# Gates of a hybrid encoder layer by Strassen's seven products

## The chip, the cores and the metric

The kernel runs on one core of one Trainium2 chip. The metric is device time in microseconds of one execution: 1601.31 us, the median of 3 runs (1599.61 to 1603.38). The engines are TensorE (PE; its weight loads are listed as PEld), VectorE (DVE), ScalarE (ACT), GpSimd (POOL) and SyncE (SP, which here only issues transfers).

## The reference

One layer over L = 1040 tokens (16 meta tokens and 1024 real ones) of width 1024, float32. What matters here:

```python
a = rms_norm(h, norm_mix[l])
(q_na, k_na, v_na, q_hg, z_f, z_b, i_hg, g_hg, gate_na, gate_hg) = split_cols(a @ w_in[l])
y_na = neighbourhood_attention(hd(q_na), hd(k_na), hd(v_na), na_rpb[l]).reshape(B, L, NA_WIDTH) @ w_na_out[l]
y_hg = hgrn2_branch(q_hg, z_f, z_b, i_hg, g_hg, lb_all[:, l], hg_norm[l]) @ w_hg_out[l]
mix = jax.nn.sigmoid(gate_na) * y_na + jax.nn.sigmoid(gate_hg) * y_hg
h = h + mix @ w_o[l]
m = rms_norm(h, norm_mlp[l])
h = h + jnp.square(jax.nn.relu(m @ w_up[l])) @ w_down[l]
```

The two gates are 2048 of the 6144 columns of `a @ w_in`. The meta tokens' own outputs are dropped at the end, so the kernel computes the gates for the 1024 real tokens only.

## The kernel before, in words

Everything is float32 in and out. Each large product is made of three matmuls on the float32r type: an operand is split into a rounded high part and the remainder (`split`, L93: a cast on ACT, a subtraction on DVE), and high x high, high x low and low x high are summed in PSUM (`mm3`, L132). A matmul has a 128x128 stationary block and 512 moving columns.

The order of the work is: the norm of x and its transposition into `aT` (two halves of 512 tokens, each a high and a low tile of 8 blocks of 128 input rows, in the pool `up`); four heads of the HGRN2 recurrence (`hgrn`, L265); four pairs of attention heads (L501); gates and branch outputs (L626 to L674); the product with W_o (L693 to L777); the MLP's up projection, already by seven products in Winograd's form (L892 to L937); the MLP's down projection and the final norm.

In the heads, projections of a 128-column block of w_in (`proj_steps`: 2 x 24 matmuls and 2 evacuations) are put between the levels of the recurrence's tree, in which DVE and POOL make the next level's operands (L360 to L364). POOL also adds `kd` (L338) and takes the root before the head's normalisation (L90, L91). Head outputs are kept in `oT` (L454), attention outputs in `OT` (L613), 16 KB per partition each, until the branch outputs split them into `sh` and `sl` (L651).

Gates (`gate_proj`, L632) are 16 column blocks of 2 x 24 matmuls, each half evacuated by a sigmoid on ACT (L636) into one of four tiles `sg`. They run two to four blocks ahead of the branch outputs, which use them: for each of 8 output blocks and 2 halves, 12 matmuls and then a multiplication by the gate (L670; L672 and L673 for the second branch).

Outside the down projection (which is written with a manual order) the framework orders each engine's instructions by readiness and by place in the program, and a tile that takes another's space waits for it. Raw weights, high and low parts of blocks live in the pool `wp` with two slots each. The high and low tiles of W_o (`wrp`) take space at the right end once `oT`, `OT`, `sh` and `sl` are given back, and `mT`, the split of `mix`, lies in the space of `aT`. PSUM has 8 banks: two `mm` banks throughout and six that `psum_pools` deals out again at each stage. All loads and nearly all stores are issued by SP in one queue.

Of the kernel before, what the change touches and what calls it, by code (L numbers as in the profile page):

```python
# [18 lines left out]
P = 128  # L19
# [27 lines left out]
def layer(ctx: ExitStack, tc: tile.TileContext, x, meta, w_in, w_na, w_hg, w_o, w_up, w_dn,  # L47
# [129 lines left out]
    def proj(*args, **kw):  # L177
        for _ in proj_steps(*args, **kw):
            pass
# [85 lines left out]
    def hgrn(hd, hp, lmask_get, gates, more):  # L265
# [3 lines left out]
        def tmp(name):  # L269
            return hp.tile([P, TH], F32, tag="tmp", name=name, bufs=4)  # L270

# [158 lines left out]
        for hf in (1, 0):  # L430
            po = pos[hf] = bank("b", "po")
            for c in range(3, -1, -1):
# [3 lines left out]
                if g < 7:  # L436
                    pe.matmul(po[:, c], QQ[:, 0, g * P:(g + 1) * P], SB[:, g], start=False, stop=True)
        list(more)
        yield
        for hf in (1, 0):  # L440
            po = pos[hf]
            sq = tmp("sq").rearrange("p (c v) -> p c v", v=P)
            act.activation(sq, po, AF.Square)
            ss = hp.tile([P, 4], F32, tag="ss", name="ss", bufs=2)
            dve.tensor_reduce(ss, sq, axis=AX.X, op=ALU.add)
# [12 lines left out]
    with tc.tile_pool(name="hp", bufs=1, reuse_waits="tile") as hp:  # L458
# [20 lines left out]

    OTp = oTs.enter_context(tc.tile_pool(name="OTp", bufs=1, side="right", reuse_waits="tile"))  # L480
    psum_pools(mx=1, s=2, t=2, b=1)
    OT = OTp.tile([P, NPAIR, T], F32, name="OT")
    with tc.tile_pool(name="np", bufs=1, reuse_waits="tile") as npl:
# [17 lines left out]
        for p in range(NPAIR):  # L501
# [51 lines left out]

            po = {}

            def scores(s, i):
# [19 lines left out]
            def values(s, i, js, pr):  # L576
# [34 lines left out]
                dve.tensor_copy(low, ov[64:])  # L611
                dst = OT[64 * i:64 * i + 64, p].rearrange("p (r s c) -> p s r c", s=8, c=8)
                dve.tensor_tensor(dst[:, s - 3:s + 1], ov[:64].rearrange("p s (r c) -> p s r c", c=8),  # L613
# [8 lines left out]
            for st in pend:  # L622
                values(*st)


    psum_pools(mx=3, a=3)  # L626
# [5 lines left out]
    def gate_proj(col):  # L632
        sg = sgp.tile([P, T], F32, tag="sg", name="sg")

        def ev(ps, t0, n):
            act.activation(sg[:, t0:t0 + n], ps, AF.Sigmoid)  # L636
        proj(col, ev)
        return sg

    gates = []  # L640

    def gates_to(n):
        for m in range(len(gates), min(n, 2 * KC)):
            gates.append(gate_proj((C_GH if m < KC else C_GN) + (m % KC) * P))

    for br, (wsrc, src) in enumerate(((w_hg, oT), (w_na, OT))):
        with tc.tile_pool(name="op", bufs=1, reuse_waits="tile") as op_:
            sh = op_.tile([P, 4, T], F32R, name="sh")
            sl = op_.tile([P, 4, T], F32R, name="sl")
            gates_to(8 * br + 2)  # L650
            for k in range(4):  # L651
                split(sh[:, k], sl[:, k], src[:, k])
            for jj in range(0, KC, 2):
                gates_to(8 * br + jj + 4)
                raw = wp.tile([P, KC, P], F32, tag="raw", name="raw").rearrange("p a b -> p (a b)")
                hi = wp.tile([P, KC, P], F32R, tag="hi", name="hi").rearrange("p a b -> p (a b)")
                lo = wp.tile([P, KC, P], F32R, tag="lo", name="lo").rearrange("p a b -> p (a b)")
                sp.dma_start(raw.rearrange("p (k c) -> p k c", k=4),
                             wsrc[:, jj * P:(jj + 2) * P].rearrange("(k p) c -> p k c", p=P))
                split(hi, lo, raw)  # L660
                for j in (jj, jj + 1):
                    sg = gates[8 * br + j]
                    for h in range(2):
                        pm = mm_tile()
                        t = slice(h * TH, (h + 1) * TH)
                        for k in range(4):
                            c = slice(k * 2 * P + (j - jj) * P, k * 2 * P + (j - jj + 1) * P)
                            mm3(pm, hi[:, c], lo[:, c], sh[:, k, t], sl[:, k, t], k == 0, k == 3)
                        if br == 0:
                            dve.tensor_tensor(mix[:, j, t], pm, sg[:, t], op=ALU.mult)  # L670
                        else:
                            dve.tensor_tensor(sg[:, t], pm, sg[:, t], op=ALU.mult)  # L672
                            dve.tensor_tensor(mix[:, j, t], mix[:, j, t], sg[:, t], op=ALU.add)  # L673
    oTs.close()  # L674

# [42 lines left out]
    for i in range(8):  # L718
# [4 lines left out]

    NP = DFF // (2 * P)
    dramp = ctx.enter_context(tc.tile_pool(name="dramp", bufs=1, space=bass.MemoryType.DRAM))
# [5 lines left out]
    def winograd(eng, a11, a12, a21, a22, s1, s2, s3, s4):  # L735
        eng.tensor_tensor(s1, a21, a22, op=ALU.add)
        eng.tensor_tensor(s2, s1, a11, op=ALU.subtract)
        eng.tensor_tensor(s3, a11, a21, op=ALU.subtract)
        eng.tensor_tensor(s4, a12, s2, op=ALU.subtract)

# [54 lines left out]

    def chain(ps, lhs, rhs, first):

        for k in range(4):
            c = slice(k * P, (k + 1) * P)
            pe.matmul(ps, lhs[0][:, c], rhs[0][:, k], start=first and k == 0, stop=False, skip_group_check=True)  # L800
            pe.matmul(ps, lhs[0][:, c], rhs[1][:, k], start=False, stop=False, skip_group_check=True)  # L801
            pe.matmul(ps, lhs[1][:, c], rhs[0][:, k], start=False, stop=k == 3, skip_group_check=True)  # L802


    w_pools = [upa]

    def weights(src):
# [5 lines left out]
        return hi, lo  # L813

    def up_bank(t):
        return bank(t, t).rearrange("p a b -> p (a b)")

# [388 lines left out]
```

## Time and profile before

| | |
|---|---|
| median of 3 runs | 1601.31 us (1599.61 to 1603.38) |
| profiled execution | 1602.57 us, of which the span (first to last instruction) is 1600.4 us |
| mean granted TensorE clock | 0.997 |
| PE / DVE / ACT / POOL busy | 1555.2 / 964.2 / 607.6 / 333.9 us |
| heads | about 40 to 390 us |
| attention | about 390 to 616 us |
| gates and branch outputs | about 616 to 862 us |
| W_o | about 864 to 957 us |
| up projection | about 960 to 1288 us |

Times in the profile are from the span's start. In a group's row stand line, engine, operation, output<-inputs and count, then busy time and the mean of one in ns, then the idle time before it and what ended it. In a row of the timeline stand start, duration and, in brackets, the idle time before it and what ended that. Matmuls overlap, so their pace is read from the distance of their starts.

### The profile page before, as it was taken

Reading aid. Unit: us, or ns where it says so; the run is one execution under the profiler, and the core shown is the slowest. Engines: PE = TensorE matmul, PEld = TensorE weight load, DVE = VectorE, ACT = ScalarE, POOL = GpSimd, SP = SyncE. Lnnn points to the kernel's source line nnn. Section 1 sums busy time; section 2 is a strip of 40 time slices with the busy share of each in tenths; the row PEclk is TensorE's granted clock in tenths of the full one; section 3 lists DMA queues with packets and bytes.
Section 4 is the critical chain, followed back from the end, with each engine's and each line's share of the span. In section 5 each row is a group of like instructions: output and inputs, shape, how many; then the busy total and the mean of one; then the engine's idle time right before and its main releaser. Section 6 shows DMA issues by size and latency. Waiting matters only on the chain.

```text
span 1600.4 us, 20348 instructions
## 1 busy us (share of the span) xinstructions
PE 1555.2 (97%) x7876; PEld 1309.3 (82%) x7876; DVE 964.2 (60%) x1524; ACT 607.6 (38%) x1082; POOL 333.9 (21%) x299
## 2 busy tenths in 40 slices
PE   6999999999999999999999998999999999999998
PEld 5788889888888888888887876788888878887886
DVE  6666767565767865123226258766666454779666
ACT  6221121112656654112123035555555443434444
POOL 4322121212011000000000012543333300227033
PEclk9999999999999999999999999999999999999999
DMA  5101001002122111111412123544444477563324
GB/s 184 40 27 40 27 28 40 27 28 68 30 74 63 45 41 40 40 53 53 145 53 78 54 105 113 168 156 163 145 152 145 160 261 234 199 224 118 99 86 145
DMA packets 120625, 158.03 MB, mean 99 GB/s; under 512 B 6337, under 2 KB 80065, under 8 KB 120529
## 3 DMA queue, kind: packets, MB, share of 16 engines
q1 hardware_dynamic: 118624, 150.70, 28.7%
q10 hardware_dynamic: 1584, 4.98, 0.8%
q8 instruction: 62, 1.02, 0.3%
q0 software_dynamic: 320, 1.05, 0.2%
q14 instruction: 35, 0.28, 0.1%
HBM read 118.96 MB, written 37.75 MB: 98 GB/s over the span
## 4 chain that ended last, share of the span: by engine, by line
PE 86%; DVE 7%; issue 3%; ACT 2%; POOL 1%; DMA 1%; DVEq 0%; POOLq 0%; SPq 0%; ACTq 0%
PE mm L134 14%; PE mm L133 13%; PE mm L135 13%; PE mm L949 4%; PE pa L949 4%; PE pc L949 4%; PE sc L351 4%; PE pb L949 3%; PE pb L800 3%; PE pb L802 3%; PE pb L801 3%; PE pc L800 2%; PE pc L801 2%; PE pc L802 2%; PE pa L800 2%
## 5 line engine op out<-in xcount | busy, mean ns | idle before, releaser
L133 PE MATMUL mm<-aT,hi 128*128 128x512 f32 (+2 forms) x896 | 328.6, 367 | 1.2 <-DVE QX L507 1.2
L135 PE MATMUL mm<-aT,lo 128*128 128x512 f32 (+2 forms) x896 | 327.5, 366 | 0.1
L134 PE MATMUL mm<-aT,hi 128*128 128x512 f32 (+2 forms) x896 | 326.6, 364 | 0.0
L133 PEld LDWEIGHTS mm<-aT,hi 128*128 128x128 f32 x896 | 169.6, 189 | 23.5 <-issue 1.4
L135 PEld LDWEIGHTS mm<-aT,lo 128*128 128x128 f32 x896 | 169.4, 189 | 23.1 <-POOL lo L124 0.3
L134 PEld LDWEIGHTS mm<-aT,hi 128*128 128x128 f32 x896 | 169.5, 189 | 22.0
L95 DVE TENSOR_TENSOR dl<-ur,dh 128x1024 fp32r<-128x1024 f32 x55 | 76.5, 1392 | 93.7 <-ACT dh L94 91.8
L94 ACT CAST dh<-ur 128x1024 fp32r<-128x1024 f32 x55 | 57.9, 1053 | 162.3 <-issue 78.1
L123 ACT CAST hi<-raw 128x1024 fp32r<-128x1024 f32 x44 | 46.3, 1053 | 189.0 <-PE mm L134 171.2
L124 DVE TENSOR_TENSOR lo<-raw,hi 128x1024 fp32r<-128x1024 f32 x42 | 51.6, 1230 | 85.8 <-ACT hi L123 85.8
L90 POOL TENSOR_SCALAR rtm<-ssq 128x1 f32<-128x1 f32 (+1 forms) x17 | 7.5, 439 | 397.0 <-ACT junk L754 372.1
L812 DVE TENSOR_TENSOR wl<-sx,wh 128x512 fp32r<-128x512 f32 x70 | 50.0, 722 | 30.7 <-ACT wh L811 30.7
L811 ACT CAST wh<-sx 128x512 fp32r<-128x512 f32 x70 | 42.6, 620 | 64.9 <-PE pc L801 27.3
L812 DVE TENSOR_TENSOR wl<-raw,wh 128x512 fp32r<-128x512 f32 x46 | 50.2, 1091 | 23.8 <-ACT wh L811 23.0
L351 PE MATMUL sc<-QQ,X 128*128 128x128 f32 x448 | 61.7, 288 | 1.5 <-DVE QQ L378 1.2
L351 PEld LDWEIGHTS sc<-QQ,X 128*128 128x128 f32 x448 | 58.2, 196 | 4.4 <-issue 2.0
L363 POOL TENSOR_TENSOR Y<-X,TN 128x512 f32<-128x512 f32 x20 | 33.8, 1691 | 110.3 <-DVE X L360 110.3
L819 ACT ACTIVATE uv<-uv 128x512 f32<-128x512 f32 x48 | 30.4, 633 | 66.4 <-DVE uv L927 49.9
L932 POOL TENSOR_TENSOR us<-u,uv 128x512 f32<-128x512 f32 x15 | 24.3, 1619 | 137.5 <-ACT uv L820 137.5
L569 DVE CUSTOM_DVE_ANT_0 pr<-nsc,NB 128x432 f32<-128x432 f32 (+1 forms) x64 | 35.3, 559 | 28.1 <-PE nsc L564 27.9
L800 PE MATMUL pb<-nt,wh 128*128 128x512 f32 x128 | 50.3, 393 | 2.0 <-DVE uv L920 2.0
L551 POOL TENSOR_TENSOR NB<-NB,bs 128x256 f32<-128x256 f32 (+1 forms) x24 | 19.6, 842 | 156.3 <-DMA NB<-in_wmask 94.1
(331 smaller groups left out, 3906.3 us busy)
## 6 DMA issues: line engine op xcount, KB each, us to landing
ur<-usp SPq DMA_DIRECT2D x55, 512.0 KB, 3.3
raw<-in_w_in SPq DMA_DIRECT2D x48, 512.0 KB, 3.7
raw<-in_w_up SPq DMA_DIRECT2D x16, 1024.0 KB, 6.0
usp<-us SPq DMA_DIRECT2D x60, 256.0 KB, 2.1
w<-in_w_dn SPq DMA_DIRECT2D x16, 512.0 KB, 4.5
usp<-uv SPq DMA_DIRECT2D x30, 256.0 KB, 2.5
xt<-in_x SPq DMA_DIRECT2D x8, 512.0 KB, 9.3
hres<-in_x SPq DMA_DIRECT2D x8, 512.0 KB, 6.5
```

Source lines behind the costliest of these rows:

```text
L94: act.copy(hi, src)
L95: dve.tensor_tensor(lo, src, hi.bitcast(F32), op=ALU.subtract)
L124: eng.tensor_tensor(lo[:, :kc], raw[:, :kc], hi[:, :kc].bitcast(F32), op=ALU.subtract)
L133: pe.matmul(ps, lh, rh, start=first, stop=False)
L134: pe.matmul(ps, lh, rl, start=False, stop=False)
L135: pe.matmul(ps, ll, rh, start=False, stop=last)
L351: pe.matmul(sc[:, c], X[:, tb + c * P:tb + (c + 1) * P], fap(QQ, tb + c * P, [[2 * h, P // (2 * h)], [T + h, 2], [1, h]]), start=True, sto ...
L800: pe.matmul(ps, lhs[0][:, c], rhs[0][:, k], start=first and k == 0, stop=False, skip_group_check=True)
L801: pe.matmul(ps, lhs[0][:, c], rhs[1][:, k], start=False, stop=False, skip_group_check=True)
L802: pe.matmul(ps, lhs[1][:, c], rhs[0][:, k], start=False, stop=k == 3, skip_group_check=True)
L812: dve.tensor_tensor(v(lo), src, v(hi).bitcast(F32), op=ALU.subtract)
L949: pe.matmul(ps, a[n == 2][:, q, j * P:(j + 1) * P], b[n == 1][:, q], start=first and n == 0, stop=last and n == 2, skip_group_check=True)
```

## The change

**Gates.** The gate matrix (1024 inputs x 2048 outputs) is taken in 8 pairs of 128-column blocks. For a pair, inputs are halved (rows 0 to 511 and 512 to 1023), as are outputs (the pair's two blocks) and tokens (two halves of 512), which makes a 2x2 by 2x2 product of blocks; it is computed with seven block products in Winograd's form, 12 matmuls each, instead of eight. Products 1 and 2 of every pair use plain halves of `a` (`first_gates`); the result of product 1 is kept in `g1`, and the two together are one quarter of the output. The other five (`gate_pair`) use sums of weights, made per pair on DVE (`gate_sums`), and sums of `a`, named t1 to t4. PSUM is dealt as pa, pb and pc, two banks each.

**Sums of `a`.** They are made on POOL, head by head, inside the recurrence (`block_sums`, after the head's last matmuls), from high plus low of the blocks, and stored in DRAM. In the gate stage they are loaded again and split (`second_operand`); t2 takes the place of one quarter of `a`, which is no longer needed.

**Gate results** are no longer kept until used: each quarter is stored in DRAM by a transfer issued on ACT's queue behind the sigmoid (`gate_out`), and loaded by SP in the branch outputs.

**Branch outputs** of the heads and the attention go to DRAM too (the tile `oT` and the large `OT` are gone), and are loaded and split (`branch_operand`) into the space of `a`, after all gates instead of between them. Matmuls, multiplications and weights of the branch outputs stay as they are. `tmp` in the heads has 6 slots instead of 4.

```diff
-    oTs = ExitStack()
-    oTp = oTs.enter_context(tc.tile_pool(name="oTp", bufs=1, side="right"))
-    oT = oTp.tile([P, NHG, T], F32, name="oT")
+    def block_sums(k, pool_):
+        r = {}
+        for v, h, kk in (("t1", 0, k), ("t3", 1, k), ("t2", 1, k + 4), ("t4", 0, k + 4)):
+            r[v] = pool_.tile([P, TH], F32, tag="tmp", name="rt", bufs=6)
+            hi, lo = (t[:, kk, :TH].bitcast(F32) for t in aT[h])
+            pool.tensor_tensor(r[v], hi, lo, op=ALU.add)
+        pool.tensor_tensor(r["t1"], r["t3"], r["t1"], op=ALU.subtract)
+        pool.tensor_tensor(r["t3"], r["t2"], r["t3"], op=ALU.subtract)
+        pool.tensor_tensor(r["t2"], r["t2"], r["t1"], op=ALU.subtract)
+        pool.tensor_tensor(r["t4"], r["t4"], r["t2"], op=ALU.subtract)
+        for v in r:
+            sp.dma_start(tsp[v][k], r[v])
...
         list(more)
+        block_sums(hd, hp)
         yield
...
-            dve.scalar_tensor_tensor(oT[:, hd, hf * TH:(hf + 1) * TH], pt.rearrange("p c t -> p (c t)"),
+            ot = hp.tile([P, TH], F32, tag="ot", name="ot", bufs=2)
+            dve.scalar_tensor_tensor(ot, pt.rearrange("p c t -> p (c t)"),
...
+            sp.dma_start(osp[0][hd][:, hf * TH:(hf + 1) * TH], ot)
...
+            sp.dma_start(osp[1][p], OT)
...
+    def gate_out(c, h, t, src):
+        act.activation(t, src, AF.Sigmoid)
+        act.dma_start(gsp[c][:, h * TH:(h + 1) * TH], t)
+
+    def first_gates(ms):
+        blocks, ps = [], []
+        for m in ms:
+            hi, lo = load_block(w_in[:, gate_col(2 * m):gate_col(2 * m) + P], KC)
+            blocks.append([[flat(t)[:, q * TH:(q + 1) * TH] for t in (hi, lo)] for q in range(2)])
+        for m, b in zip(ms, blocks):
+            ps.append(mm_tile())
+            chain(ps[-1], b[0], aV["b11"], True)
+            act.copy(g1[m], ps[-1])
+        for m, b, p in zip(ms, blocks, ps):
+            chain(p, b[1], aV["b21"], False)
+            gate_out(2 * m, 0, gfp.tile([P, TH], F32, tag="go", name="go", bufs=2), p)
+
+    psum_pools(pa=2, pb=2, pc=2)
+    first_gates((0, 1))
+    first_gates((2, 3))
...
+    def second_operand(v):
+        for k in range(4):
+            t = g_tile("gv", TH, bufs=5)
+            sp.dma_start(t, tsp[v][k])
+            split(aV[v][0][:, k], aV[v][1][:, k], t)
+
+    def gate_weights(src):
+        w_turn[0] ^= 1
+        n = src.shape[1]
+        hi, lo = (wp.tile([P, KC, P], F32R, tag=t, name=t) if w_turn[0] else
+                  gp.tile([P, KC, P], F32R, tag=t, name=t, bufs=2) for t in ("hi", "lo"))
+        hi, lo = flat(hi)[:, :n], flat(lo)[:, :n]
+        split(hi, lo, src)
+        return [[t[:, q:q + TH] for t in (hi, lo)] for q in range(0, n, TH)]
+
+    def gate_sums(m):
+        raw = []
+        for q in range(2):
+            t = (wp.tile([P, KC, P], F32, tag="raw", name="raw") if m % 2 == 0 else
+                 gp.tile([P, KC, P], F32, tag="raw", name="raw", bufs=2))
+            c = gate_col(2 * m + q)
+            sp.dma_start(t, w_in[:, c:c + P].rearrange("(k p) c -> p k c", p=P))
+            raw.append(flat(t))
+        sa, sb = g_tile("sx", D, bufs=2), g_tile("sx", D, bufs=2)
+        winograd(dve, raw[0][:, :TH], raw[0][:, TH:], raw[1][:, :TH], raw[1][:, TH:],
+                 sb[:, :TH], sa[:, TH:], sb[:, TH:], sa[:, :TH])
+        W = {}
+        W["s4"], W["s2"] = gate_weights(sa)
+        W["s1"], W["s3"] = gate_weights(sb)
+        W["a22"], = gate_weights(raw[1][:, TH:])
+        return W
+
+    def gate_pair(m, W, before):
+        pb, pc = up_bank("pb"), up_bank("pc")
+        p3 = g_tile("p3", TH, bufs=2)
+        chain(pc, W["s4"], aV["b22"], True)
+        act.copy(p3, pc)
+        before()
+        chain(pb, W["s2"], aV["t2"], True)
+        u1, u3, u2 = (g_tile("gv", TH, bufs=5) for _ in range(3))
+        dve.tensor_tensor(u1, pb, g1[m], op=ALU.add)
+        chain(pc, W["s1"], aV["t1"], False)
+        dve.tensor_tensor(u1, u1, pc, op=ALU.add)
+        gate_out(2 * m, 1, u1, u1)
+        chain(pb, W["s3"], aV["t3"], False)
+        dve.tensor_tensor(u3, pb, g1[m], op=ALU.add)
+        pool.tensor_tensor(u3, u3, p3, op=ALU.subtract)
+        dve.tensor_tensor(u3, u3, pc, op=ALU.add)
+        gate_out(2 * m + 1, 1, u3, u3)
+
+        def last():
+            chain(pb, W["a22"], aV["t4"], False)
+            dve.tensor_tensor(u2, pb, g1[m], op=ALU.add)
+            gate_out(2 * m + 1, 0, u2, u2)
+        return last
+
+    W = gate_sums(0)
+    first_gates((4, 5))
+    for v in ("t2", "t1"):
+        second_operand(v)
+    first_gates((6, 7))
+    for v in ("t3", "t4"):
+        second_operand(v)
+    last = lambda: None
+    for m in range(NG):
+        last = gate_pair(m, W, last)
+        if m + 1 < NG:
+            W = gate_sums(m + 1)
+    last()
...
+    osrc = [u_tiles(br, "o") for br in range(2)]
+    def branch_operand(br):
+        for k in range(4):
+            raw = wp.tile([P, KC, P], F32, tag="raw", name="raw")
+            sp.dma_start(flat(raw), osp[br][k])
+            split(*(t[:, 2 * k:2 * k + 2, :TH] for t in osrc[br]), raw.rearrange("p (h a) b -> p h (a b)", h=2))
+
+    branch_operand(0)
+    for br, wsrc in enumerate((w_hg, w_na)):
+        for jj in range(0, KC, 2):
...
+            if br == 0 and jj == 2:
+                branch_operand(1)
+            for j in (jj, jj + 1):
+                sg = sgp.tile([P, T], F32, tag="sg", name="sg")
+                sp.dma_start(sg, gsp[8 * br + j])
```

`chain` (12 matmuls: 4 input blocks times three), `winograd` (four sums) and `up_bank` are the functions that the up projection had; they are defined earlier now.

More of the change, by code (lines that the diff above doesn't have):

```diff
@@ L623, in layer, with winograd, chain @@
                 values(*st)
+            sp.dma_start(osp[1][p], OT)
+    def winograd(eng, a11, a12, a21, a22, s1, s2, s3, s4):
+        eng.tensor_tensor(s1, a21, a22, op=ALU.add)
+        eng.tensor_tensor(s2, s1, a11, op=ALU.subtract)
+        eng.tensor_tensor(s3, a11, a21, op=ALU.subtract)
+        eng.tensor_tensor(s4, a12, s2, op=ALU.subtract)
+    def chain(ps, lhs, rhs, first):
+        for k in range(4):
+            c = slice(k * P, (k + 1) * P)
+            pe.matmul(ps, lhs[0][:, c], rhs[0][:, k], start=first and k == 0, stop=False, skip_group_check=True)
+            pe.matmul(ps, lhs[0][:, c], rhs[1][:, k], start=False, stop=False, skip_group_check=True)
+            pe.matmul(ps, lhs[1][:, c], rhs[0][:, k], start=False, stop=k == 3, skip_group_check=True)
@@ L626, in layer @@
+    W = gate_sums(0)
[11 more added lines that the diff above has]
+    last()
+    gps.close()
+    gfs.close()
     psum_pools(mx=3, a=3)
@@ L646, in layer @@
[L646 to L673, printed above, removed]
@@ L794, in a_tile @@
         return pool_.tile([P, n], dt, tag=tag, name=tag, bufs=bufs)
[L796 to L802, printed above, removed]
     w_pools = [upa]
```

67 lines of the change are left out of this document (44 added, 23 removed).

## The prediction

> **What bounds the kernel now.** I read the engine totals of the page and its chain of waits first, then the busy time stage by stage, then the order of instructions inside the stage that the change rewrites.
>
> ```profile
> span 1600.4 us, 20348 instructions
> PE 1555.2 (97%) x7876; PEld 1309.3 (82%) x7876; DVE 964.2 (60%) x1524; ACT 607.6 (38%) x1082; POOL 333.9 (21%) x299
> ...
> PE 86%; DVE 7%; issue 3%; ACT 2%; POOL 1%; DMA 1%; DVEq 0%; POOLq 0%; SPq 0%; ACTq 0%
> ```
>
> TensorE is the chain for 86% of the span. A busy TensorE need not be at its rate, so the stages and the spacing of matmuls come next (columns of the stages: length, PE, PEld, DVE, ACT, POOL with counts, granted clock, DMA share, GB/s).
>
> ```profile
> 640.00:760.00 120.00, 120.00 (x531) 99.41 (x530) 28.73 (x31) 23.10 (x30) 0.00 (x0) 1.00 0.16 49
> 760.00:866.00 106.00, 104.86 (x463) 86.36 (x462) 42.45 (x58) 25.40 (x37) 0.00 (x0) 1.00 0.24 80
> ...
> 1060.00:1120.00 60.00, 60.00 (x266) 49.69 (x266) 37.82 (x49) 31.02 (x54) 24.16 (x17) 1.00 0.46 157
> ...
> 1300.00:1400.00 100.00, 100.00 (x442) 82.61 (x441) 58.12 (x66) 39.90 (x53) 10.66 (x7) 1.00 0.66 231
> ```
>
> ```profile
> 742.64 0.39 PE L133 MATMUL mm<-sh,hi 128*128 128x512 f32 x1
> ...
> 745.36 0.39 PE L133 MATMUL mm<-sh,hi 128*128 128x512 f32 x1
> ```
>
> The two starts are 12 matmuls apart: 2.72 us, so one 128x512 matmul costs 0.2267 us, whatever the 0.39 us in its row. Gates and branch outputs (640 to 866) are that stream without a hole, at granted clock 1.00, with DVE 24 to 40% busy, ACT 19 to 24%, and POOL empty. A matmul taken out there is time taken out, as long as nothing new makes TensorE wait. The stage at 1060 is the up projection, which has the structure that the gates will get (seven products, L892 to L937), with DVE 63% and ACT 52% busy, and it too has no hole.
>
> **The change, part by part.** *Products.*
>
> ```profile
> L636 ACT ACTIVATE sg<-mm x32: 587/598/601, 615.6 to 841.5; 128x512 f32<-128x512 f32 x32
> ```
>
> 32 half-columns of 24 matmuls are 768. After: 8 pairs of 7 products of 12 are 672. 96 x 0.2267 = **-21.8 us**. The 384 matmuls of the branch outputs stay.
>
> The Trainium skill, "TensorE: Matmul & The Clock Gate", section "Back-to-back issue gap", gives about 131 ns for a sustained N=512 matmul; by it the saving would be an estimated 12.6 us. The 227 ns of the trace is used.
>
> *One pair in steady state.* 5 products remain in it (two are done ahead), 13.6 us of TensorE.
>
> ```profile
> L124 DVE TENSOR_TENSOR lo<-raw,hi x42: 1207/1224/1586, 46.2 to 820.3; 128x1024 fp32r<-128x1024 f32 x42
> L736 DVE TENSOR_TENSOR sx<-raw x16: 679/692/1661, 987.0 to 1238.2; 128x512 f32<-128x512 f32 x16
> L94 ACT CAST wh<-raw x8: 1045/1048/1053, 862.5 to 884.4; 128x1024 fp32r<-128x1024 f32 x8
> L94 ACT CAST mT<-mix x16: 610/620/623, 835.8 to 865.5; 128x512 fp32r<-128x512 f32 x16
> L912 ACT COPY p<-pc x16: 568/580/588, 995.3 to 1269.8; 128x512 f32<-128x512 f32 x16
> L753 ACTq DMA_DIRECT2D hsp<-hres x8: 326/326/337, 915.3 to 957.3; - x8
> ```
>
> DVE: 4 weight sums and 5 evacuations at 0.69, splits of 2 x 1.22 and 0.69: 9.4 us, 69%. ACT: casts 2 x 1.05 and 0.62, one copy 0.58, 3 sigmoids at 0.60, 3 store issues at 0.33: 6.1 us, 45%. A store issued on ACT follows the sigmoid that it stores, so it holds the ACT queue for little more than its issue. This is the load that the up projection carries without a hole, with one POOL operation instead of five. Cost 0; if cover fails, each evacuation that is late costs TensorE about the 2 us seen at 1016 below.
>
> *The start of the stage.* While the first products of blocks 2 to 7 run (6 x 5.44 = 32.6 us; blocks 0 and 1 fill the gaps of the attention's end as the first gate did before), DVE has 6 block splits (7.3), 16 operand splits at 0.69 (11.0) and the first sums and their splits (5.9): 24 us. ACT has 6 x (1.05 + 0.58 + 0.60 + 0.33) + 16 x 0.62 + 2.7 = 28 us. It fits, but two things are narrow. A block's second product ends 2.72 us before its slot's next user must be ready, against sigmoid, cast and the low part (0.60 + 1.05 + 1.22 = 2.9 us). And the pool of two split slots is shared: two of the three splits of the first sums take both slots and hold them until products 3, 5 and 7 of pair 0, so blocks 4 to 7 wait, and pair 0 must run before them, on raw weights whose load starts only when two raw slots are free (3.7 us to landing) and then 2.8 us of sums. The nearest row is the start of the up projection:
>
> ```profile
> raw<-in_w_in SPq DMA_DIRECT2D x48, 512.0 KB, 3.7
> ...
> 960.00:1000.00 40.00, 34.40 (x172) 27.77 (x173) 34.50 (x52) 24.08 (x46) 10.81 (x9) 0.96 0.37 113
> ```
>
> ```profile
> 989.65 0.50 PE L800 MATMUL pb<-nT,wh 128*128 128x512 f32 x1 [3.96 <-ACT wh L811]
> 990.69 0.79 PE L800 MATMUL pc<-nT,wh 128*128 128x512 f32 x1 [0.31 <-ACT wh L811]
> 1016.00 0.50 PE L800 MATMUL pb<-nt,wh 128*128 128x512 f32 x1 [1.97 <-DVE uv L920]
> ```
>
> That slice lost 5.6 of its 40 us, at a granted clock of 0.96 behind the long hole, and the wait at 1016 another 2.0: near 8. DVE was 86% busy there, with transposes that the gates don't have. Bounds 0 and 8; I take **+4.5**, half of it at the raw weights.
>
> *Sums of a.* Per head, 8 POOL operations on 128x512 (4 of hi+lo, 4 differences), then 4 stores on SP. The rows are a group, a wait of POOL, the second head's stage and the lengths (min/median/max) of one DVE line.
>
> ```profile
> L363 POOL TENSOR_TENSOR Y<-X,TN 128x512 f32<-128x512 f32 x20 | 33.8, 1691 | 110.3 <-DVE X L360 110.3
> ...
> POOL st L90 <- DVE ss L445: 120.6, 8, 32.0
> ...
> 155.00:240.00 85.00, 84.46 (x527) 75.22 (x526) 57.93 (x105) 16.66 (x32) 18.91 (x20) 1.00 0.11 32
> ...
> L361 DVE TENSOR_TENSOR X<-X,TN x20: 673/685/1526, 63.8 to 347.9; 128x512 f32<-128x512 f32 x20
> ```
>
> 8 x 1.69 = 13.5 us per head, 54 in all. POOL is 18.9 busy in 85 and once per head idle up to 32.0 us (before L90), so the 13.5 fits. Queued behind it on POOL stand the root before the head's normalisation (L90, L91), the kd sum and the level steps (L338, L363), whose results DVE and TensorE wait for; one operation in the wrong place delays these by 1.7 us, and projections fill. L361 shows a DVE operation stretched from 0.69 to 1.53 us; if all of a head's 13.5 us stretched DVE, it would be 71 of 85 and still not the bound. On SP, weight loads stand behind stores that wait for POOL, but a block is loaded one block (48 matmuls, 10.9 us) ahead. In the first head, before TensorE has projections enough, less is covered. Bounds 0 and 54; by the idle row nearly all hides: **+1.5**.
>
> The Trainium skill, "SBUF — State Buffer", section "Who interferes with whom", says that a VectorE instruction with two SBUF inputs and a GpSimd instruction that reads SBUF block each other whole. The 1.53 us in L361 agrees. It speaks against these sums, and is the third rival's reason.
>
> *Outputs through DRAM.* oT and OT become stores (8 of 256 KB, 4 of 512 KB) and 8 loads of 512 KB into freed space of a; their splits are those made before. Gates add 32 stores of 256 KB and 16 loads of 512 KB. In the branch outputs (384 x 0.2267 = 87 us) this is 12.6 MB more, 145 GB/s on top of 49 to 80: about what the stage at 1300 moves (231) with TensorE full. The gate for the first output can be loaded only after the last product has left its space, 3.7 us like the raw weights, against five banks of 2.72 each. Cost 0; uncovered, one load, 3.7.
>
> *The seam to W_o.* Weights of W_o waited for the space of sh and sl, until the last branch matmul:
>
> ```profile
> 862.09 0.39 PE L135 MATMUL mm<-sh,lo 128*128 128x512 f32 x1
> 863.62 1.43 PE L133 MATMUL mm<-wh,mT 128*128 128x512 f32 x5 [1.14 <-ACT wh L94]
> 872.67 0.50 PE L133 MATMUL mm<-wh,mT 128*128 128x512 f32 x1 [0.24 <-ACT wh L94]
> 873.93 0.50 PE L134 MATMUL mm<-wl,mT 128*128 128x512 f32 x1 [0.28 <-DVE wl L95]
> ```
>
> That pool is gone, so they can be split earlier: **-1.7**, the three waits. Bounds 0 and -2.6: the first seam is 1.53 from start to start, 1.3 beyond the spacing, and some 0.3 is lost around each of the others beside its wait. New there: the second half of mT lies where the W_na operand is read to the end, so its 8 splits (8 x 0.69, 5.5 us) start only then; rows 0 to 3 of W_o (4 x 5.44 = 21.8 us) use the first half and cover it.
>
> *Table.* ACT changes from Exp to Sigmoid once, 1.28 us. Gate results no longer wait for attention's space, so a sigmoid may slip between exponentials and cost two more changes. ACT is 61% busy there:
>
> ```profile
> L636 ACT ACT_TABLE_LOAD  x1: 1283/1283/1283, 613.3 to 613.3; - x1
> ...
> 560.00:612.00 52.00, 51.95 (x309) 44.19 (x308) 37.26 (x103) 31.67 (x76) 1.90 (x3) 1.00 0.11 31
> ```
>
> With gate matmuls to fill, 0; at worst 2.6.
>
> **Sum.** -21.8 + 4.5 + 1.5 - 1.7 = -17.5: the span goes from 1600.4 to 1582.9. The profiled execution took 1602.57, 2.2 more than its span; the median of the runs is 1601.31. Taken from the median, 1583.8; I say **1583.5 us**.
>
> **The rivals.** *Second: the starved start.* The shared split slots and the late raw weights cost what the up projection's start cost, 8, and blocks 4 to 7 wait once more after pair 0 (one raw load and one split, 3.7 + 1.05 + 1.22 = 6). For it: the slot count above. Against: first products, pair 0 and the operand splits can run in any order that is ready. 1583.5 - 4.5 + 14 = 1593.
>
> *Third, slower: POOL becomes part of the chain of the recurrence.* Place: the heads, 40 to 390 us. Price: 54 us if all shows; with half, 27: 1583.5 - 1.5 + 27 = 1609. It passes the time before when more than 19.3 of the 54 us (36%, three of a head's eight operations) stand ahead of a waited-for POOL step or stretch DVE on the path. For it: kd and level steps follow one another with DVE in between, and the operations have no late input, so they can be issued anywhere. Against: the 32 us idle and TensorE's 84.5 of 85 with projections to fill.
>
> *Fourth: everything hides* and the seam gains fully: 1601.3 - 21.8 - 2.6 = 1577.
>
> **Chances.** Forecast 0.62 (its own range 1578 to 1589), starved start 0.18, slower 0.08, all hidden 0.12. The range takes in the first, most of the second and the fourth: 1577 to 1595. This kernel's measurement tells about 0.2%, 3.2 us, from no change. Faster by more: 0.90; within: 0.03; slower: 0.07 (nearly all of the third).
>
> **What would show it.** Matmuls of the gates 672, spaced 0.2267. From the first gate matmul after attention to the end of the branch outputs about 21.8 less, plus holes on TensorE of 4 to 5 us in the first 35 us of the gate stage, waiting for a cast, a low part or raw weights. None once pairs run. The heads still 85 us apart, POOL about 32 busy in each. No wait for wh at the first W_o row. I am wrong if heads grow apart, if pairs show holes at each evacuation (DVE or ACT late), or if branch outputs wait for DMA.

## The result, and the profile after

The changed kernel takes 1609.55 us (median of 5, 1608.22 to 1613.78), the kernel before 1601.04 us beside it (median of 5): a ratio of 1.006, 95% interval 1.004 to 1.0079. It is slower, by 8.5 us, where 17.8 less was forecast. The execution that was profiled took 1613.35 us and its span is 1611.6, 11.2 more than the span of before; its granted clock is 0.990.

Here is the page after. Beside the one of before, TensorE's share of the chain of waits falls from 86 to 83%, and DVE's rises from 7 to 9%.

```profile
span 1611.6 us, 20640 instructions
PE 1545.5 (96%) x7780; PEld 1298.8 (81%) x7780; DVE 1059.3 (66%) x1628; ACT 640.8 (40%) x1132; POOL 394.0 (24%) x339
...
PE 83%; DVE 9%; issue 3%; ACT 2%; POOL 1%; DMA 1%; DVEq 0%; POOLq 0%; SPq 0%; ACTq 0%
```

7780 matmuls stand for 7876: the 96 are gone. TensorE is busy 9.7 us less in a span that is 11.2 longer, so it stands idle some 21 us more. Where, is read by cutting both traces at the same pieces of work: the last write of a head's output, the last score of the attention, the first and the last W_o matmul (starts; the differences are of unrounded times).

| stretch | before | after | difference |
|---|---|---|---|
| start to the end of the heads | 385.2 | 404.6 | +19.3 |
| to the attention's last scores | 220.0 | 220.8 | +0.9 |
| to the first W_o matmul (gates, branch outputs) | 258.4 | 248.4 | -10.0 |
| to the last W_o matmul | 92.6 | 90.8 | -1.8 |
| to the end | 644.2 | 647.0 | +2.8 |

**The heads.** These are the stages of the first three heads (length, busy time of PE, PEld, DVE, ACT, POOL with counts, granted clock, DMA share, GB/s).

```profile
70.00:155.00 85.00, 79.74 (x473) 70.33 (x473) 58.67 (x100) 13.82 (x28) 30.79 (x28) 0.97 0.11 34
155.00:240.00 85.00, 80.13 (x498) 71.46 (x497) 58.39 (x99) 15.93 (x31) 25.77 (x26) 0.98 0.15 48
240.00:325.00 85.00, 80.12 (x498) 71.30 (x497) 61.27 (x103) 14.61 (x30) 25.20 (x24) 0.98 0.16 50
```

Before, the second of these windows had 84.46 of 85 busy on TensorE; now 80.1. POOL, at 25 to 31 of 85, is still no bound. What counts is the order on it. First the timeline of POOL before, around the last two levels of a head, then the same place after (start, duration, line, operation, idle before).

```profile
85.07 1.48 POOL L363 TENSOR_TENSOR Y<-X,TN 128x512 f32<-128x512 f32 x1 [2.80 <-DVE X L360]
92.74 1.46 POOL L363 TENSOR_TENSOR Y<-X,TN 128x512 f32<-128x512 f32 x1 [6.19 <-DVE X L360]
```

```profile
84.54 1.48 POOL L381 TENSOR_TENSOR Y<-X,TN 128x512 f32<-128x512 f32 x1 [2.82 <-DVE X L378]
85.98 6.52 POOL L232 TENSOR_TENSOR rt<-aT,aT 128x512 f32<-128x512 f32 x4
92.47 1.72 POOL L234 TENSOR_TENSOR rt<-rt 128x512 f32<-128x512 f32 x1
94.27 1.33 POOL L235 TENSOR_TENSOR rt<-rt 128x512 f32<-128x512 f32 x1
95.68 1.62 POOL L236 TENSOR_TENSOR rt<-rt 128x512 f32<-128x512 f32 x1
97.38 1.28 POOL L237 TENSOR_TENSOR rt<-rt 128x512 f32<-128x512 f32 x1
98.61 1.07 POOL L381 TENSOR_TENSOR Y<-X,TN 128x512 f32<-128x512 f32 x1
...
140.30 0.20 POOL L90 TENSOR_SCALAR st<-ss 128x4 f32<-128x4 f32 x1 [33.51 <-DVE ss L464]
```

All eight operations of the head stand in one row between two level steps, 12.6 us of work in a place where POOL had waited 6.2. The step (L381) starts 14.07 us behind the one before it instead of 7.67, and is 0.39 shorter: 6.0 us late. The 33.5 us of idle time, in which the sums would have held up no step, come afterwards and are untouched.

The step's input is late too, though less. DVE's copy into `X`, for which POOL waited before, ends 9.94 us behind the level step ahead of it instead of 7.59, because DVE's operations take longer while POOL makes sums. One of them, before and after:

```profile
88.05 1.23 DVE L124 TENSOR_TENSOR lo<-raw,hi 128x1024 fp32r<-128x1024 f32 x1 [0.16 <-ACT hi L123]
```

```profile
87.51 2.12 DVE L124 TENSOR_TENSOR lo<-raw,hi 128x1024 fp32r<-128x1024 f32 x1 [0.16 <-ACT hi L123]
```

So the late input alone accounts for 2.35 of the 6.4 us by which the step starts late; the queue on POOL makes it 6.4.

TensorE pays where it needs what is made from that step: its waits for `QQ` in the heads (us in total, times, longest), before, after, and the longest of them in the timeline:

```profile
PE sc L351 <- DVE QQ L378: 1.2, 4, 0.3
```

```profile
PE sc L369 <- DVE QQ L396: 14.5, 10, 3.5
...
101.63 3.52 PE L369 MATMUL sc<-QQ,X 128*128 128x128 f32 x16 [3.46 <-DVE QQ L396]
```

Cut from the first level step of the second head to that of the third, the price of one head is (before, after):

```profile
143.03:228.16 85.13, 84.59 (x528) 75.34 (x527) 57.93 (x106) 16.66 (x32) 18.91 (x20) 1.00 0.11 32
```

```profile
149.31:240.94 91.63, 86.76 (x528) 76.91 (x527) 63.10 (x106) 16.53 (x32) 30.40 (x28) 0.98 0.15 46
```

The head is 6.5 us longer with the same 528 matmuls: TensorE is idle 4.3 us more, and its matmuls, at a granted clock of 0.98, take 2.2 more.

**The start of the gates.** Stages and holes after the attention:

```profile
640.00:660.00 20.00, 15.76 (x64) 11.83 (x63) 12.70 (x18) 10.42 (x17) 0.00 (x0) 0.96 0.87 274
660.00:680.00 20.00, 18.97 (x79) 14.73 (x78) 13.16 (x19) 9.64 (x16) 1.61 (x1) 0.96 0.61 187
700.00:720.00 20.00, 20.00 (x90) 16.56 (x89) 14.02 (x19) 7.00 (x10) 2.90 (x2) 1.00 0.48 146
800.00:870.00 70.00, 70.00 (x310) 57.98 (x309) 43.44 (x59) 13.62 (x16) 0.00 (x0) 1.00 0.71 243
```

```profile
635.11 0.52 PE L606 MATMUL ppt<-ident,pr 128*128 128x128 f32 x3 [1.75 <-DVE PT L618]
637.17 0.50 PE L664 MATMUL mm<-aT,hi 128*128 128x512 f32 x1 [0.55 <-ACT g L697]
648.62 0.50 PE L664 MATMUL pc<-aT,hi 128*128 128x512 f32 x1 [1.62 <-ACT hi L94]
...
658.67 0.79 PE L664 MATMUL pc<-at,hi 128*128 128x512 f32 x1 [1.86 <-ACT at L94]
```

Summed over the starts of the 512-column matmuls in the 80 us behind the attention's last scores, 10.4 us are lost beyond the spacing of 0.2267 (idle time, and slow matmuls behind it at a granted clock of 0.96), and 1.75 more at the transpose of 635: **12.2 us**, where the same 80 us of before lose 0.5. Then nothing: pairs and branch outputs run full (0.2 us lost up to the first W_o matmul), with DMA at 243 GB/s from 800 to 870 us.

### The profile page after: what moved, and what is told of

The parts are those of the page before. It is cut to its first block, busy times and chain, and to the rows that moved or that the text cites. A ratio compares the mean times of both kernels' runs of the same rounds, so it can differ in the third digit from the quotient of the medians.

```text
span 1611.6 us, 20640 instructions
## 1 busy us (share of the span) xinstructions
PE 1545.5 (96%) x7780; PEld 1298.8 (81%) x7780; DVE 1059.3 (66%) x1628; ACT 640.8 (40%) x1132; POOL 394.0 (24%) x339
## 3 DMA queue, kind: packets, MB, share of 16 engines
q0 software_dynamic: 320, 1.05, 0.2%
## 4 chain that ended last, share of the span: by engine, by line
PE 83%; DVE 9%; issue 3%; ACT 2%; POOL 1%; DMA 1%; DVEq 0%; POOLq 0%; SPq 0%; ACTq 0%
PE mm L133 10%; PE mm L134 10%; PE mm L135 10%; PE mm L1080 4%; PE pa L1080 4%; PE pb L664 4%; PE pb L666 4%; PE pb L665 4%; PE pc L1080 4%; PE pb L1080 3%; PE sc L369 3%; PE pc L664 3%; PE pc L665 2%; PE pc L666 2%; PE pa L664 2%
## 5 line engine op out<-in xcount | busy, mean ns | idle before, releaser
L133 PE MATMUL mm<-aT,hi 128*128 128x512 f32 (+2 forms) x640 | 229.6, 359 | 2.3 <-DVE QX L528 2.3
L135 PE MATMUL mm<-aT,lo 128*128 128x512 f32 (+2 forms) x640 | 228.1, 356 | 0.0
L134 PE MATMUL mm<-aT,hi 128*128 128x512 f32 (+2 forms) x640 | 227.6, 356 | 0.0
L133 PEld LDWEIGHTS mm<-aT,hi 128*128 128x128 f32 x640 | 122.5, 191 | 15.2 <-issue 2.4
L135 PEld LDWEIGHTS mm<-aT,lo 128*128 128x128 f32 x640 | 121.9, 191 | 13.2
L134 PEld LDWEIGHTS mm<-aT,hi 128*128 128x128 f32 x640 | 122.1, 191 | 12.7
L94 ACT CAST dh<-ur 128x1024 fp32r<-128x1024 f32 x55 | 57.9, 1053 | 162.1 <-issue 78.1
L123 ACT CAST hi<-raw 128x1024 fp32r<-128x1024 f32 x36 | 37.8, 1051 | 114.5 <-PE mm L134 91.8
L369 PE MATMUL sc<-QQ,X 128*128 128x128 f32 x448 | 65.2, 299 | 14.5 <-DVE QQ L396 14.5
L946 DVE TENSOR_TENSOR wl<-sx,wh 128x512 fp32r<-128x512 f32 x70 | 50.1, 724 | 30.4 <-ACT wh L945 30.3
L124 DVE TENSOR_TENSOR lo<-raw,hi 128x1024 fp32r<-128x1024 f32 x34 | 43.5, 1279 | 33.9 <-ACT hi L123 33.9
L762 POOL TENSOR_TENSOR gv<-gv,p 128x512 f32<-128x512 f32 x8 | 12.2, 1530 | 191.3 <-DVE gv L761 179.3
L950 ACT ACTIVATE uv<-uv 128x512 f32<-128x512 f32 x48 | 30.4, 633 | 66.2 <-DVE uv L1058 50.0
L1170 POOL TENSOR_TENSOR w<-w,tt 128x512 f32<-128x512 f32 x16 | 23.3, 1457 | 134.0 <-DVE tt L1169 119.4
L381 POOL TENSOR_TENSOR Y<-X,TN 128x512 f32<-128x512 f32 x20 | 32.7, 1636 | 84.5 <-DVE X L378 84.5
```

The lines of the kernel that those rows point to most:

```text
L94: act.copy(hi, src)
L124: eng.tensor_tensor(lo[:, :kc], raw[:, :kc], hi[:, :kc].bitcast(F32), op=ALU.subtract)
L133: pe.matmul(ps, lh, rh, start=first, stop=False)
L134: pe.matmul(ps, lh, rl, start=False, stop=False)
L135: pe.matmul(ps, ll, rh, start=False, stop=last)
L369: pe.matmul(sc[:, c], X[:, tb + c * P:tb + (c + 1) * P], fap(QQ, tb + c * P, [[2 * h, P // (2 * h)], [T + h, 2], [1, h]]), start=True, sto ...
```

## The experiments

Each run's expectation was written before it ran. Ratios are to the kernel before, run on the same chip beside it.

| run | median us | ratio, 95% interval |
|---|---|---|
| sums late (e1) | 1590.45 | 0.9930 (0.9912 to 0.9948) |
| sums alone (e2) | 1625.29 | 1.0141 (1.0122 to 1.0160) |
| half of the sums (e3) | 1593.60 | 0.9941 (0.9922 to 0.9959) |
| sums in the attention (e4) | 1599.17 | 0.9977 (0.9967 to 0.9986) |
| first gates first (e5) | 1588.99 | 0.9921 (0.9907 to 0.9934) |
| loads first (e6) | 1588.58 | 0.9915 (0.9901 to 0.9928) |
| one table (e7) | 1587.14 | 0.9899 (0.9885 to 0.9913) |

### Sums late

```diff
-    pool.tensor_tensor(fap(KB, h, hv), ...)
+    last_pool = pool.tensor_tensor(fap(KB, h, hv), ...)
...
-        block_sums(hd, hp)
+        with tc.issue_after(last_pool.ins):
+            block_sums(hd, hp)
```

> The changed kernel, with one edit: the eight POOL operations of a head's sums are put in POOL's order behind the head's last level step (the last multiplication that makes KB) instead of directly ahead of the last Y. Number, size and operands of the operations stay, and so do the stores.
> Theory A (place in the queue: 12.6 us of ready work stand ahead of a step that DVE and TensorE wait for): the heads come back from about 91 to about 85 us each, the last scores' wait for QQ is near 1 us again instead of 3.5, TensorE is again about 84.5 busy of 85, and the time falls by 17 to 20 us, to 1590 to 1593 us.
> Rival B (contention: POOL's reading and writing of 128x512 tiles stretches DVE's operations wherever it stands): the same work still stretches DVE, and the time stays within 5 us of the changed kernel, 1604 to 1610.
> Rival C (the 16 stores of the sums on SP delay the weight loads of projections): the stores only move a few us, 1604 to 1610 too, with projections waiting for raw weights.

Measured: 1590.45 us, 19.1 less than the changed kernel (some 21 by the two ratios, each taken beside the kernel before). POOL, the waits for `QQ`, the second head's stage and a DVE row:

```profile
93.19 1.46 POOL L381 TENSOR_TENSOR Y<-X,TN 128x512 f32<-128x512 f32 x1 [6.20 <-DVE X L378]
...
102.46 5.10 POOL L232 TENSOR_TENSOR rt<-aT,aT 128x512 f32<-128x512 f32 x4
...
134.44 0.20 POOL L90 TENSOR_SCALAR st<-ss 128x4 f32<-128x4 f32 x1 [20.61 <-DVE ss L465]
...
PE sc L369 <- DVE QQ L396: 1.2, 4, 0.3
...
155.00:240.00 85.00, 84.46 (x528) 75.22 (x527) 63.60 (x106) 16.65 (x32) 29.97 (x28) 1.00 0.16 50
...
105.87 4.01 DVE L124 TENSOR_TENSOR lo<-raw,hi 128x1024 fp32r<-128x1024 f32 x1 [4.07 <-ACT hi L123]
```

The level step has its 6.2 us of idle time back, the wait for `QQ` is the 1.2 us of before, TensorE is 84.46 busy again, and the heads end at 387.3. Theory A holds. C falls, and so does B in its strong form, that the delay comes wherever the work stands: the same operations and stores, 16 us later in the queue, cost 2 us in all. But B's mechanism is there. DVE is busy 63.6 us per head instead of 57.9, and a subtraction that takes 1.22 us took 4.01 while POOL made its sums. In this place no wait of TensorE follows from it.

### Sums alone

The kernel before with the heads' part of the change (sums and their stores, which nobody reads; six `tmp` slots; head outputs through DRAM into `oT` again).

> The kernel before, with only the heads' part of the change: the sums of a on POOL with their stores (nobody reads them), six tmp slots, and head outputs stored in DRAM and loaded back into the place of oT during the attention. The gates and branch outputs are those of before.
> Theory A (the sums in the place that they have alone lengthen the heads): the heads are 18 to 20 us longer, all of it is left at the end, 1619 to 1622 us.
> Rival D (the longer heads come from something else in the change, as the space or the order that the new gates bring): the heads stay 85 us apart, 1600 to 1604.

Measured: 1625.29 us, 22.2 more than before. Its heads end at 406.4 (21.2 later), and it shows the same wait:

```profile
PE sc L369 <- DVE QQ L396: 14.5, 10, 3.5
```

Rival D falls: the new gates have no part in the longer heads.

### Half of the sums

```diff
-        pool.tensor_tensor(r["t1"], r["t3"], r["t1"], op=ALU.subtract)
-        ... (the other three differences)
```

> The changed kernel with four of the eight POOL operations of a head: the additions of high and low parts stay, the four differences are left out, so t1 to t4 are plain quarters of a and the gates are not the reference's. Place in the queue and stores stay. 6.5 us of POOL per head instead of 12.6.
> Theory A: before the change POOL stood idle for 6.2 us just ahead of that level step, so about 6.5 us of work there cost next to nothing: the heads are 0 to 1 us longer each than before, and the time is 1590 to 1594 us.
> Rival B (contention, in proportion to the work): half of the delay stays, 1598 to 1602.
> Rival C (the stores): all of it stays, 1606 to 1610.

Measured: 1593.60 us, 3.1 more than with all sums late, which the intervals do not tell apart. The level step and the one before it, then a DVE row from between them:

```profile
81.40 1.48 POOL L377 TENSOR_TENSOR Y<-X,TN 128x512 f32<-128x512 f32 x1 [2.82 <-DVE X L374]
82.84 6.52 POOL L232 TENSOR_TENSOR rt<-aT,aT 128x512 f32<-128x512 f32 x4
90.95 1.46 POOL L377 TENSOR_TENSOR Y<-X,TN 128x512 f32<-128x512 f32 x1 [1.58 <-DVE X L374]
...
84.36 2.12 DVE L124 TENSOR_TENSOR lo<-raw,hi 128x1024 fp32r<-128x1024 f32 x1 [0.16 <-ACT hi L123]
...
PE sc L365 <- DVE QQ L392: 4.2, 7, 1.2
```

The queue no longer holds the step up: 6.5 us of sums fit where POOL had waited 6.2, and the step waits for DVE again. Yet it starts 9.55 us behind the one before it instead of 7.67, 1.9 late, and DVE is why: the subtraction shown takes 2.12 instead of 1.23 us, and the next two products that make `QQ` 1.20 and 1.15 instead of 0.68, which makes up the 1.9. The heads stand 86.3 us apart instead of 85.1, so half of the work costs 1.2 us per head where all of it costs 6.5. (The end of the heads at 385.6 hides this: in this execution the first projection starts at 17.1 us, where it starts at 19.4 before.) Rival C falls once more: all the stores stand where they stood. So the price is not proportional to the work. What exceeds the idle time in that one place is paid in full (6.4 us of excess with all of the sums, 6.5 per head), and what fits is paid only as far as it holds up DVE there.

### Sums in the attention

```diff
-        block_sums(hd, hp)
...
             sp.dma_start(osp[1][p], OT)
+            block_sums(p, npl)
```

> The changed kernel with the sums of a made in the attention instead of the heads: one block per pair of attention heads, still on POOL, which has next to nothing to do there (3 instructions, 1.9 us busy in 52 us), with four slots of their own, and one slot for the pair's output instead of two.
> Theory A: the heads are as before (85 us apart); the attention stays as long, since DVE and ACT do its work; 1588 to 1593 us.
> Rival B (contention): the 50 us of POOL work now stretch the attention's DVE operations; if DVE there, 37 of 52 us busy, becomes late, the attention is longer by up to 15 us, and the time stays at 1600 to 1608.

Measured: 1599.17 us, above theory A's range and just below B's. The heads are 85.1 us apart again, as before; they end at 381.1, since in this execution the first projection starts at 16.6 us instead of 19.4. The attention's last scores come 231.6 us later instead of 220.0. At its start stand (POOL, DVE, PE):

```profile
381.90 5.05 POOL L232 TENSOR_TENSOR rt<-aT,aT 128x512 f32<-128x512 f32 x4
386.92 1.25 POOL L234 TENSOR_TENSOR rt<-rt 128x512 f32<-128x512 f32 x1
```

```profile
383.16 6.10 DVE L124 TENSOR_TENSOR lo<-raw,hi 128x1024 fp32r<-128x1024 f32 x1 [1.30 <-ACT hi L123]
...
391.89 0.56 PE L133 MATMUL mm<-aT,hi 128*128 128x272 f32 x1 [6.80 <-DVE QX L527]
```

One DVE subtraction took 6.10 us instead of 1.22, from 383.16 to 389.26, all of it while POOL made sums, and here TensorE waited 6.8 us for what stood behind it, where it waits 1.2 before. That is 5.6 of the 11.6 us; most of the rest is an estimated 5.3, from a granted clock of 0.91 over the 59 us from 381 to 440, where the first 59 us of the attention have 1.00 before. The Trainium skill, "SBUF — State Buffer", section "Who interferes with whom", says that a DVE operation with two SBUF inputs and a GpSimd operation that reads SBUF contend for a shared pair of ports, which is locked exclusively. The 6.10 and the 4.01 us agree in kind, but are longer than one POOL instruction of 1.3 us: a run of them back to back held one DVE operation for several. Contention is thus a real price of these sums, paid only where the DVE operation that it meets is on the path: not in the idle time behind a head's last level, but ahead of it (1.2 us per head with half of the sums) and at the start of the attention.

### First gates first

On top of the late sums, `W = gate_sums(0)` is moved behind the first products and the operand splits.

> The run with late sums (e1_sums_late), with one line moved: the sums of weights for pair 0 (gate_sums(0)) come in the program after the first products of blocks 4 to 7 and the operand splits, instead of before them. So pair 0's split weights no longer hold the two shared split slots while blocks 4 to 7 wait for them. Number and size of all work stay.
> In e1_sums_late the holes and slow stretches of TensorE between 616 and 680 us add up to about 10 us beyond the spacing of 0.2267 us.
> Theory E (shared slots and late first sums are the loss at the gates' start): the wait for the cast of the first weight sums (1.62 us) and of its low part go, those for blocks 4 to 7 shrink, the loss falls to 3 to 5 us, and the time falls by 4 to 7 us against e1_sums_late, to 1583 to 1587 us.
> Rival F (the loss comes from what arrives late whatever the order: DRAM loads of the sums behind the last attention store in SP's queue, and ACT's casts): the same wait comes up at another instruction, and the time stays at 1589 to 1593 us.

Measured: 1588.99 us, 1.5 less than the late sums, which the intervals do not tell apart. In the profile the loss in the 80 us behind the last scores falls from 10.0 to 6.0 us (the transpose's 1.75 in both). Of the 4 us gained, 1.0 is lost again at a wait in the branch outputs, and 1.7 in this one execution by its clock at the start of the attention, 0.97 for 56 us where the late sums had 1.00 (late sums, then this run):

```profile
384.00:440.00 56.00, 52.90 (x315) 44.97 (x314) 35.76 (x91) 32.09 (x74) 9.26 (x11) 1.00 0.21 68
```

```profile
384.00:440.00 56.00, 52.87 (x308) 45.17 (x307) 34.24 (x87) 31.10 (x71) 8.27 (x11) 0.97 0.22 68
```

The wait for the first cast of weight sums is as long as it was, only later. A stage of the start, a load on SP and the wait:

```profile
630.00:640.00 10.00, 10.00 (x46) 8.28 (x45) 5.89 (x9) 7.77 (x13) 0.00 (x0) 1.00 1.05 359
...
641.96 0.43 SPq L738 DMA_DIRECT2D raw<-in_w_in  x1
...
654.38 0.50 PE L665 MATMUL pc<-aT,hi 128*128 128x512 f32 x1 [1.61 <-ACT hi L94]
```

Theory E has part of it: the waits for weights of blocks 4 to 7 are gone. For the rest rival F's reading fits: from 626 to 656 us the DMA engines are busy nearly all the time (shares of 0.90 to 1.00 in stretches of 10 us, up to 1.05 at 359 GB/s). That some load is then late in any order is argued; the next run tries another order. The Trainium skill, "DMA: Bandwidth & Descriptors", section "Where 436 GB/s comes from", gives about 358 GB/s as what HBM lets one core have; the 359 of the trace agree.

### Loads first, and one table

Pair 0's raw weights get slots in the gate pool and are loaded ahead of the sums of `a`; its splits take one shared slot instead of two.

```diff
+    raw0 = gate_loads(0)
     first_gates((4, 5))
-    for v in ("t2", "t1"):
-        second_operand(v)
+    second_operand("t2")
+    W = gate_sums(raw0)
+    second_operand("t1")
     first_gates((6, 7))
```

> The run with late sums (e1_sums_late), with the start of the gate stage put in order of need: raw weights of pair 0 lie in slots of their own in the gate pool (the parity of the raw slots is turned), and are loaded ahead of the first products of blocks 4 to 7 and of the 16 loads of sums; their split begins in the gate pool's slots, so pair 0 holds one of the two shared slots instead of two; the sums of weights come in the program between the splits of t2 and t1. All work is the same in number and size.
> From the run with the first gates first (e5_first_gates_first): there, from 626 to 650 us, DMA moved 320 to 359 GB/s, the raw weights of pair 0 were issued on SP at 642 to 644 us behind 13 loads of sums, landed at 650, and TensorE waited 1.6 us for the first cast at 654 us.
> Theory G (order of the loads in a start that the loads limit): pair 0 can run from about 640 us, the holes between 618 and 680 us beyond the spacing fall from 5 (there) and 9 (with late sums) to 2 to 3 us, and the time to 1584 to 1587 us.
> Rival F (ACT's and DVE's chain of casts and low parts is what is late): holes stay at 4 us or more at other instructions, the time at 1587 to 1591 us.

The second edit keeps the sigmoids of blocks 0 and 1 behind the attention's last exponential:

```diff
+            if late:
+                act.copy(go, p)
+                with tc.issue_after(last_exp[0].ins):
+                    gate_out(2 * m, 0, go, go)
```

> The run with loads first (e6_loads_first), with one more edit: the first two gate results (blocks 0 and 1, second product) are copied from PSUM by ACT with a plain copy, and their sigmoid and store come behind the attention's last exponential. In the runs so far a sigmoid stood between the attention's exponentials, so ACT loaded tables four times in the attention and the gates (1.28 us each) instead of twice, and TensorE waited 1.75 us for a transposed block's low part (PT) at the attention's end.
> Theory H (the table changes make that wait): two table loads instead of four, the 1.75 us become less than 0.5 us, and the time falls by 1 to 2 us against e6_loads_first.
> Rival I: the wait has another cause (DVE's queue), or the two copies (1.2 us) cost what the tables gain: no change, within 0.5 us.

Measured: 1588.58 and 1587.14 us. The table loads of the changed kernel (first two rows) and of the last run:

```profile
L593 ACT ACT_TABLE_LOAD x2 | 2.6, 1283 | 0.0
L685 ACT ACT_TABLE_LOAD x2 | 2.6, 1283 | 0.0
```

```profile
L595 ACT ACT_TABLE_LOAD x1 | 1.3, 1283 | 0.0
L687 ACT ACT_TABLE_LOAD x1 | 1.3, 1283 | 0.0
```

Theory H holds in the trace: two loads fewer, and the 1.75 us wait at the transpose is gone (0.94 at 616 us, for a cast of weights, is new). The gain of 1.4 us in time is of the expected size, but within the spread of the runs. Of Theory G little holds, and rival F's range was met: with the loads first the loss is 6.4 us, with one table 5.5, after 6.0 with the first gates first. Pair 0 is nearly in time (0.8 us of waits for its weights), but the largest wait, beside the transpose's 1.75, is now another (PE, then ACT, loads first):

```profile
PE mm L665 <- ACT g L698: 2.0, 2, 1.5
...
644.64 2.60 ACT L94 CAST at<-gv 128x512 fp32r<-128x512 f32 x4 [1.71 <-DMA gv<-tsp_t]
647.14 0.58 ACT L698 COPY g<-mm 128x512 f32<-128x512 f32 x1
```

The copy that frees a PSUM bank stands in ACT's queue behind casts that wait 1.71 us for a load of the sums. That is akin to the event in the heads: what is waited for stands in the queue behind what is not due, here behind work that can't even run yet. It was not taken out. The last run, 1587.14 us, beats the kernel before by 1.0% (0.9 to 1.15%) and the changed kernel by some 22 us (26 by the ratios).

## Why the prediction was wrong

**Sums of a: the step that failed.** The prediction wrote "by the idle row nearly all hides: +1.5". Measured: +19.3 in the heads, all but 2 of it gone when the sums stand elsewhere in the queue. The idle row was read rightly (32.0 us before L90, and 33.5 after the change), and so was the list of what stands behind on POOL. The load was priced rightly: about 32 us of POOL per head were forecast and 30.4 measured. The error was to let the largest idle time of the engine stand for the place of the work. The operands are ready from the start, so nothing ties the operations to that idle time; the order on the queue decides, and it put them into the 6.2 us ahead of the last level step. The row for that place was to be had: POOL's timeline of before, 6.19 us of idle time against 12.6 of work, 6.4 too many. The last level steps of the four heads come 5.9, 12.4, 18.9 and 25.8 us late: the first three heads pass their delay on in full, and only behind the fourth do projections cover what it adds (191 instructions of TensorE stand between its last step and its output, 228 before). The heads growing apart, 91.6 us instead of 85.1, was one of the prediction's own signs of being wrong. "One operation in the wrong place" was the case thought of; all eight went there.

The third rival named this mechanism and place, "the operations have no late input, so they can be issued anywhere", with 8 chances in 100 and a price of 27 us. The price was 19.3. Its time of 1609 was met by luck: its price was 7.7 us too high for the heads, and the gates' start lost 7.2 more than its sum had. Its other half, DVE stretched by POOL, happened too (5 to 6 us of DVE per head). It made the level step's input 2.35 us late, which the longer queue on POOL covered, and was off the path behind the step.

**Products: right.** 96 matmuls are gone, and pairs and branch outputs run without a hole: 21.8 us of matmuls were saved.

**Outputs through DRAM: 0, right.** From the end of the gates' start to the first W_o matmul 0.2 us are lost.

**The start: +4.5, measured 12.2 - 0.5 = 11.7,** beyond its upper bound of 8. Of these, 1.75 are the transpose's and belong to the table below; the rest is beyond the bound too. The prediction had two of the causes, the shared slots and the late raw weights, and priced them by the start of the up projection. What it did not price is that the sums too are loaded only once the attention ends (with the blocks that are due, 16 x 256 KB and 4 x 512 KB, 6.3 MB, 17.5 us at 359 GB/s), and that ACT's queue holds ready work behind those loads. Over the runs the loss falls from 12.2 to 5.5 us: 2.2 went with the heads' delay, by a way that was not followed up, and 4.0 by the order of the first gates; 0.4 came back with the loads first, and 0.9 went with the tables.

**Table: 0, at worst 2.6.** The worst case came, two more table loads, with a wait of 1.75 us that went away with them.

**The seam: -1.7, measured about -3.1.** No W_o matmul waits for `wh` any more: 1.3 at the first row, and 1.8 inside (92.6 to 90.8).

**The balance.** Against the forecast span of 1582.9: heads +17.8, gates and branch outputs +8.6 (-10.0 instead of -21.8 + 4.5 - 1.3), attention +0.9, W_o -1.4, and +2.8 behind W_o, where nothing was changed: 28.7, the 1611.6 of the profile. The 2.8 go with the clock of this one execution, not with the edit: in the first 40 us behind the last W_o matmul and the next 60 it was granted 0.91 and 0.97, before 0.96 and 1.00. The run with one table has the same 0.91 and 0.97 and the same 646.8, the runs with late sums, first gates first and loads first have 644.2 to 644.5. The median lies 3.8 below the profiled execution. Without the error in the heads the forecast's range would have held: the late sums take 1590.45, near the second rival's 1593.

## What to carry to other kernels

Idle time of an engine covers added work only if the work stands in that idle time: find the gap at the very place in the queue where the work will be put, and compare its length with the whole block of work, not with one operation. Even work that fits can hold up another engine's operations that run beside it. Work whose inputs are ready early needs an explicit place, behind the last step of the critical chain, or an order that moves it anywhere may put it in front. When a stage starts from empty buffers, add up the bytes that it must load before its first full pace and order the loads by need.

## What was not expected of the hardware

A run of POOL operations on 128x512 tiles held single DVE subtractions of 1.22 us for 4.01 and 6.10 us; the prediction had seen 0.69 become 1.53. In the heads with the late step the granted clock was 0.97 to 0.98 where it is 0.99 to 1.00 with the sums late, so waits of 3.5 us on TensorE can be paid twice, the second time in slower matmuls; and after one and the same wait of 2.26 us for `QX` it was 1.00 in one execution and 0.97 in another (late sums, then first gates first), which makes 1.7 us of difference that no edit made. The wait in the late sums; in the other run the row differs in its start alone, 393.21:

```profile
393.51 0.36 PE L133 MATMUL mm<-aT,hi 128*128 128x272 f32 x1 [2.26 <-DVE QX L529]
```

Finally, 243 GB/s in the branch outputs cost TensorE nothing, while the gates' start, at up to 359 (first gates first), waited for its loads.
